# A diffusion block with three mixers: gate 1 in four column groups per step, gate 2 on VectorE, retention's heads in turn

## The chip, the cores and the metric

The kernel runs on one core of a Trainium2 chip. The metric is device time in microseconds (us), from the start to the end of one execution. Five engines work side by side on their own instruction queues: TensorE (PE in the profile; PEld is its weight load), VectorE (DVE), ScalarE (ACT), GpSimd (POOL) and SyncE (SP), which issues nearly all the DMAs here.

## What is computed

One block of a diffusion transformer for 256 latent and 256 context tokens of width 2048, in float32, shortened:

```python
m_lat = split(silu(c) @ ada_w + ada_b, 6)        # shift 1, scale 1, gate 1, shift 2, scale 2, gate 2
a_lat = modulate(x, norm1_g, m_lat[0], m_lat[1]) @ w_in      # a_ctx likewise for the context
hy, q, k, v, g, u = split_proj(a_lat)
mix = concat([hyena(hy), silu(g) * rms(retention(q, k, v)), s5(u)]) @ w_out
h = x + m_lat[2] * mix                                       # gate 1
up = modulate(h, norm2_g, m_lat[3], m_lat[4]) @ w_up         # shift 2, scale 2
gate, val = split(up, 2)
h = h + m_lat[5] * ((gelu(conv3x3(gate)) * val) @ w_down)    # gate 2
out = rmsnorm(h, norm_f)
```

Retention has eight heads of 64 query and key features and 128 value features. The modulation `ada_w` is a matrix of 2048 by 12288; its product with one vector takes no reuse of the weights at all.

## The kernel before

Weights come in blocks of 512 KB, 256 rows by 512 columns, into pages of 4 KB per partition. `split_w` (L449) loads a block, ACT rounds it to the high part (L454), DVE subtracts to get the low part (L456), and `prod` (L460) makes three PE products (L461 to L463) of each piece: high by high, high by low, low by high. Most blocks give 24 matmuls of 128 x 256 (blocks for keys of the context and for values also 128 x 512). PE cannot start on a block's second third before L456 is done. Pages for raw blocks, high and low parts and the modulation's loads are four rings of few pages each (the numbers in `RN`, and `resize`): a load into a page waits until the page's last reader is done.

Around the blocks runs other work, cut into steps by Python generators (`_Task`, L195). After each block a function `during_kv`, `during_g`, `during_hy` or `with_ada` asks each task for so many steps (`RK`, `RV`, `RG`, `RH`, `RW`, `RF`; broken rates add up). A timeline in the build then orders each engine's instructions by priority and its own estimate of when they can run; on the chip each engine goes through its list strictly in order.

One task is `ada25` (L443): the four chunks of the modulation that are needed late, 2048 columns each, in the order gate 1, shift 2, scale 2, gate 2 (chunks 0 to 3). Each takes 32 loads of 512 KB. A chunk in `ADV` goes to `ada_vector` (L419): DVE multiplies a load of 128 x 1024 with the vector's element on each partition and adds it to a sum (L428 for the first, L430 for the 15 others of a half), and PE sums over the partitions at the end of each half (L435). Any other chunk goes to `ada_matmul` (L404): PE multiplies the vector, 32 columns wide with the value in the first, into 512 columns of weights at a time (L412). The four groups of 512 columns lie side by side, on 32 of PE's columns and 32 partitions of one bank each. `ada_store` copies the sums out, transposes them (L397) and adds the bias (L400).

The order of the stages: S5 input and norm 1; keys and values of retention (with the S5 scan beside them); gates and queries; the hyena inputs, with retention's heads and the first part of hyena beside them; the output projection, 32 blocks, whose last quarter of each sum needs hyena's result; gate 1 and the residual (L1342); norm 2 (L311 to L321, L1354 to L1356 for the modulation by scale 2 and shift 2); and the feed-forward net (FFN): 11 groups of 512 gate columns (8 blocks), the convolution by nine taps on ACT and DVE (L1388, L1396), 512 value columns (8 blocks), their product (L1403) and its split in two parts (L466, L467), and the products down, which add gate 2 times the sum to the residual (L1419). The first product down comes after the third group up.

In before, gate 1 is made on PE from 163 us on, shift 2 and scale 2 on DVE from 333 to 558, gate 2 on PE from 576 to 728, all by L412 and L430 in the spaces between.

Retention (L1150) goes over four pairs of heads: per head two score matmuls into one bank (L1158, 64 rows of PE's 128, the lower for the first head of a pair and the upper for the second), the decay on DVE (L1161), the values (L1164).

Of the kernel before, what the change touches and what calls it, by code (L numbers as in the profile page):

```python
# [16 lines left out]
P = 128  # L17
D = 2048
KT = D // P
L = 256  # L20
# [36 lines left out]
def _lay(i):  # L57
    """The inputs as the kernel reads them: slices, transposes and constants of the shapes."""
# [70 lines left out]
    s = np.arange(256)  # L129
# [13 lines left out]
    # constants of the shapes  # L143
# [24 lines left out]
RN=[2,3,3,3];SA=40000;SF=30000;R0=10;R1=1;R2=1;RS=4;RK=2;RV=3;RG=.8;RH=.8;RW=.75;RF=.8;RT=1.2;RR=3;RY=.75;PR=500;ADV=[1,2];ORD=[0,1,2,3];RP=1.5;RQ=20;KS=5;PW=800;AR=[6,8,8,8,7,5,5,5];ZE=[1,3];VE=[0,1,3];UE=[1,3]  # L168
class _Pages:
    """Tags of fixed sizes in the slot pool, taken and given back in the order of the program."""  # L170
# [12 lines left out]
class _Ring:  # L183
    """Tags taken in turn."""
# [9 lines left out]
class _Task:  # L194
    """Work that is emitted piece by piece between the blocks of the large products."""  # L195
# [23 lines left out]
def tile_dit(ctx: ExitStack, tc: tile.TileContext, I, out: bass.AP, dbg=None):  # L219
# [15 lines left out]
    def stream(name, start):  # L235
        """Instructions whose order of priority starts at -start and goes on from use to use."""
# [9 lines left out]
    def resize(kind, n):  # L246
        """A ring of n pages of 4 KB."""
        tags = ring[kind].tags
        while len(tags) < n:
            tags.append(pages.take(4))  # L250
        while len(tags) > n:
            pages.give(tags.pop())
# [53 lines left out]
    def sum_squares(ps, sq, first, last):  # L306
        """Sums over the partitions and parts of sq [P, n, w], a token on each partition."""
# [6 lines left out]
    def inv_rms(ps, n, w):  # L314
        """1/sqrt(sum/n + eps) of w tokens' sums, on all partitions."""
# [76 lines left out]
    def ada_store(c, ps):  # L392
        """Four rows of 512 columns to their places."""
# [10 lines left out]
    def ada_matmul(c):  # L404
        """2048 of the modulation's columns for the latents, as products of TensorE."""
        ps = ada_bank()
        for kt in range(KT):
            raw = [load_a(I["ada25"][c, kt, half]) for half in range(2)]
            for half in (1, 0):
                for e in range(2):  # L410
                    q = 2 * half + e
                    T.matmul(ps[32 * q:32 * q + 32, :], cs[:, kt, :], raw[half][:, e, :],  # L412
                             start=(kt == 0), stop=(kt == KT - 1), skip_group_check=True)
                if (kt, half) != (KT - 1, 0):
                    yield
# [1059 lines left out]
```

## Time and profile before

| | us |
|---|---|
| median of three executions | 1503.16 |
| lowest, highest | 1502.71, 1507.03 |
| the profiled execution | 1507.03 |
| its span, first to last instruction | 1506.4 |
| PE busy in it | 1459.1 |
| DVE busy | 1040.6 |
| ACT busy | 658.0 |

The profiled execution is the highest of the three. The mean granted clock of TensorE was 0.987 of full speed. A row of the profile names line, engine, operation, output and inputs with shapes and how many; lengths are those of the records, which overlap a little on one engine, while the busy time of a window counts overlapping records once. A matmul in float32 leaves two records, a matmul of the split parts one. The idle time in brackets is the engine's idle time ahead of that row with what ended it.

### The profile page before, as it was taken

What the parts mean: (1) busy time and instruction counts of PE and PEld (TensorE: products, weight loads), DVE (VectorE), ACT (ScalarE), POOL (GpSimd) and SP (SyncE); (2) the same over time, 40 slices, a digit from 0 to 9 for tenths busy, and PEclk for the clock granted to TensorE, in tenths of its full rate; (3) what the DMA queues carried; (4) which work ended last, traced back from release to release, by engine and by line L of the source; (5) the groups of instructions that cost most, each with busy time, mean ns of one, the idle gap of its engine ahead of it and who ended that gap; (6) DMA issues with size and microseconds to landing.
All of it is one profiled execution on the core that took longest, in us unless ns stands there. A gap on an engine that the chain in (4) does not pass through costs nothing.

```text
span 1506.4 us, 27320 instructions
## 1 busy us (share of the span) xinstructions
PE 1459.1 (97%) x11180; PEld 1314.7 (87%) x11180; DVE 1040.6 (69%) x1772; ACT 658.0 (44%) x974; POOL 10.9 (1%) x9
## 2 busy tenths in 40 slices
PE   6998999999999999999999999999999999999997
PEld 3566687678888987788899999999999999999997
DVE  6579519897869887653777665775667577657756
ACT  6337741213576433232554443443444344434434
POOL 0000000000000000000000000000000000000000
PEclk9999999999999999999999999999999999999998
DMA  9788635568877887677465666556665666656562
GB/s 352 260 313 291 229 101 197 183 194 278 281 252 253 299 303 261 219 226 251 145 182 183 185 182 184 185 177 192 183 183 182 182 183 183 185 183 184 178 189 90
DMA packets 89956, 318.58 MB, mean 211 GB/s; under 512 B 12039, under 2 KB 12584, under 8 KB 89384
## 3 DMA queue, kind: packets, MB, share of 16 engines
q1 hardware_dynamic: 89832, 316.85, 65.4%
q8 instruction: 87, 1.43, 0.4%
q14 instruction: 37, 0.30, 0.1%
HBM read 312.62 MB, written 4.19 MB: 210 GB/s over the span
## 4 chain that ended last, share of the span: by engine, by line
PE 83%; DVE 7%; DMA 5%; ACT 3%; issue 1%; SPq 0%; DVEq 0%; ACTq 0%
PE mm L461 24%; PE mm L462 23%; PE mm L463 23%; DMA s4k<-in_ada_dram 4%; PE ad L412 4%; DVE s4k L456 1%; DVE s4k L430 1%; PE sm L852 1%; PE ad L373 1%; PE sm L576 1%; PE mm L339 1%; PE sm L546 1%; DMA s4k<-in_x_t_dram 1%; PE sm L1158 0%; PE sm L1164 0%
## 5 line engine op out<-in xcount | busy, mean ns | idle before, releaser
L456 DVE TENSOR_TENSOR s4k<-s4k,s4k 128x1024 fp32r<-128x1024 f32 x376 | 459.6, 1223 | 324.1 <-ACT s4k L454 300.5
L454 ACT CAST s4k<-s4k 128x1024 fp32r<-128x1024 f32 x376 | 393.8, 1048 | 654.7 <-PE mm L462 483.3
L462 PE MATMUL mm<-s4k,s4k 128*128 128x256 f32 (+1 forms) x2144 | 629.0, 294 | 1.5 <-DVE s4k L775 1.2
L461 PE MATMUL mm<-s4k,s4k 128*128 128x256 f32 (+1 forms) x2144 | 626.9, 295 | 3.5 <-ACT s4k L454 3.1
L463 PE MATMUL mm<-s4k,s4k 128*128 128x256 f32 (+1 forms) x2144 | 624.7, 294 | 3.2 <-DVE s4k L456 3.2
L461 PEld LDWEIGHTS mm<-s4k,s4k 128*128 128x128 f32 x2144 | 411.9, 193 | 27.3 <-issue 12.9
L462 PEld LDWEIGHTS mm<-s4k,s4k 128*128 128x128 f32 x2144 | 414.3, 193 | 18.4 <-issue 8.2
L463 PEld LDWEIGHTS mm<-s4k,s4k 128*128 128x128 f32 x2144 | 412.1, 193 | 17.2 <-issue 6.9
L461 PE MATMUL mm<-s8k,s4k 128*128 128x256 f32 x960 | 272.7, 285 | 0.0
L462 PE MATMUL mm<-s8k,s4k 128*128 128x256 f32 x960 | 271.7, 284 | 0.0
L463 PE MATMUL mm<-s8k,s4k 128*128 128x256 f32 x960 | 271.1, 284 | 0.0
L461 PEld LDWEIGHTS mm<-s8k,s4k 128*128 128x128 f32 x960 | 183.9, 192 | 14.4 <-issue 12.6
L463 PEld LDWEIGHTS mm<-s8k,s4k 128*128 128x128 f32 x960 | 183.7, 192 | 4.3 <-issue 3.4
L462 PEld LDWEIGHTS mm<-s8k,s4k 128*128 128x128 f32 x960 | 184.3, 192 | 2.7 <-issue 2.5
L1396 DVE SCALAR_TENSOR_TENSOR t<-mm,s4k,t 128x189 f32<-128x189 f32 (+2 forms) x352 | 131.9, 424 | 7.9 <-ACT t L1388 6.3
L430 DVE SCALAR_TENSOR_TENSOR s4k<-s4k,cs,s4k 128x1024 f32<-128x1024 f32 x60 | 76.8, 1280 | 21.0 <-DMA s4k<-in_ada_dram 20.4
L412 PE MATMUL ad<-s4k,cs 128*32 128x512 f32 x256 | 62.7, 612 | 1.0 <-DMA s4k<-in_ada_dram 1.0
L1419 DVE SCALAR_TENSOR_TENSOR s4k<-mm,ada_cols,s4k 128x256 f32<-128x256 f32 x96 | 39.9, 477 | 4.7 <-PE mm L463 4.7
L373 PE MATMUL ad<-s4k,cs 128*32 128x256 f32 x512 | 35.6, 392 | 4.7 <-DMA s4k<-in_ada_dram 4.0
L1388 ACT ACTIVATE t<-mm,s4k 128x256 f32<-128x256 f32 x44 | 24.7, 562 | 14.6 <-PE mm L463 13.6
L466 ACT CAST s8k<-t 128x512 fp32r<-128x512 f32 x38 | 23.0, 616 | 18.2 <-DVE t L1403 9.3
L373 PEld LDWEIGHTS ad<-s4k,cs 128*32 128x32 f32 x512 | 13.8, 110 | 19.1 <-DMA s4k<-in_ada_dram 5.7
(281 smaller groups left out, 1023.5 us busy)
## 6 DMA issues: line engine op xcount, KB each, us to landing
s4k<-in_ada_dram SPq DMA_DIRECT2D x192, 512.0 KB, 4.9
s4k<-in_w_up_dram SPq DMA_DIRECT2D x176, 512.0 KB, 3.7
s4k<-in_w_down_dram SPq DMA_DIRECT2D x88, 512.0 KB, 3.7
s4k<-in_w_in_dram SPq DMA_DIRECT2D x80, 512.0 KB, 4.9
s4k<-in_w_out_dram SPq DMA_DIRECT2D x32, 512.0 KB, 4.6
s4k<-in_x_t_dram SPq DMA_DIRECT2D x8, 512.0 KB, 6.6
s4k<-in_ctx_t_dram SPq DMA_DIRECT2D x4, 512.0 KB, 10.2
hyk<-s8k SPq DMA_DIRECT2D x4, 512.0 KB, 4.0
```

The lines of the kernel that those rows point to most:

```text
L373: T.matmul(ps[32 * q:32 * q + 32, :], cs[:, 2 * k2 + e, :], raw[:, e, 256 * part:256 * part + 256], start=(k2 == 0), stop=(k2 == 7), skip_ ...
L412: T.matmul(ps[32 * q:32 * q + 32, :], cs[:, kt, :], raw[half][:, e, :], start=(kt == 0), stop=(kt == KT - 1), skip_group_check=True)
L430: V.scalar_tensor_tensor(acc, raw, cs[:, kt, 0:1], acc, ALU.mult, ALU.add)
L454: S.copy(h, raw)
L456: V.tensor_tensor(lo, raw, h.bitcast(F32), ALU.subtract)
L461: T.matmul(ps, a[0], b[0], start=first, stop=False, skip_group_check=True)
L462: T.matmul(ps, a[0], b[1], start=False, stop=False, skip_group_check=True)
L463: T.matmul(ps, a[1], b[0], start=False, stop=last, skip_group_check=True)
L466: S.copy(h, src)
L1388: S.activation(acc[:, e, :], at(m), AF.Identity, bias=cw[:, 9, mt:mt + 1], scale=cw[:, 4, mt:mt + 1])
L1396: V.scalar_tensor_tensor(dst[:, r0:r1, c0:c1], src[:, r0 + dy:r1 + dy, c0 + dx:c1 + dx], cw[:, tap, mt:mt + 1], dst[:, r0:r1, c0:c1], ALU. ...
L1419: V.scalar_tensor_tensor(h_of(mt), at(m), ada_cols[:, 3, mt:mt + 1], h_of(mt), ALU.mult, ALU.add)
```

## The change

Three edits in the code, and numbers in the parameter line. `ada_matmul` issues all four column groups of a row tile in one step, from two loads, and hands back control once per row tile (16 steps) instead of once per load (32). `ADV` takes chunk 3, gate 2, to DVE. Retention takes a second bank per pair of heads and issues the scores so that the two heads take turns. Of the numbers, `RN` gives the modulation three pages instead of two in the stage of keys and values; a `resize` afterwards takes it back to two before gates and queries. `RK` goes from 2 to 1, `RV` from 3 to .5 and `RW` from .75 to .85, with which gate 1's 16 steps come beside the 24 blocks of keys and values, 8 beside the keys and 8 beside the values. Comments are left out too, which moves line numbers: L412 becomes L410, L428 and L430 become L426 and L428, L454 and L456 become L452 and L454.

```diff
-RN=[2,3,3,3]; ... RK=2;RV=3; ... RW=.75; ... ADV=[1,2];
+RN=[3,3,3,3]; ... RK=1;RV=.5; ... RW=.85; ... ADV=[1,2,3];
...
             raw = [load_a(I["ada25"][c, kt, half]) for half in range(2)]
-            for half in (1, 0):
-                for e in range(2):
-                    q = 2 * half + e
-                    T.matmul(ps[32 * q:32 * q + 32, :], cs[:, kt, :], raw[half][:, e, :],
-                             start=(kt == 0), stop=(kt == KT - 1), skip_group_check=True)
-                if (kt, half) != (KT - 1, 0):
-                    yield
+            for q in range(4):
+                T.matmul(ps[32 * q:32 * q + 32, :], cs[:, kt, :], raw[q // 2][:, q % 2, :],
+                         start=(kt == 0), stop=(kt == KT - 1), skip_group_check=True)
+            if kt < KT - 1:
+                yield
...
+    resize("ada", 2)
     tag_sg = pages.take(8)
...
             yb = sm_bank()
+            pss = [sm_bank(), sm_bank()]
+            for s in range(2):
+                for e in range(2):
+                    ph = slice(64 * e, 64 * e + 64)
+                    T.matmul(pss[e][:, L * s:L * s + L], k_t[ph, pr, 128 * s:128 * s + 128], q_t[ph, pr, :],
+                             start=True, stop=True)
             for e in range(2):
                 hd = 2 * pr + e
-                ph = slice(64 * e, 64 * e + 64)
-                ps = sm_bank()
-                for s in range(2):
-                    T.matmul(ps[:, L * s:L * s + L], k_t[ph, pr, 128 * s:128 * s + 128], q_t[ph, pr, :],
-                             start=True, stop=True)
+                ps = pss[e]
```

With the four chunks' steps changed in number (128 before, 112 after), they also fall on other stages: gate 1 alone goes with keys and values, shift 2 and scale 2 with gates, queries, hyena and the output projection, and gate 2 with the first two groups up of the FFN.

Where the instructions stand is told by each engine's list. The first place is on DVE in the FFN, before: the end of the first group up (L1403 and L467) and, from the row that ends in `s4k_1066_7697` on, the split of the blocks of the second group up.

```order
L1396 SCALAR_TENSOR_TENSOR t_7304<-mm_7027,s4k_989_7022,t_7304 128x3x63
L1403 TENSOR_TENSOR t_7284<-t_7284,mm_7324 128x512
L456 TENSOR_TENSOR s4k_1064_7669<-s4k_1062_7665,s4k_1063_7667 128x1024
L1403 TENSOR_TENSOR t_7304<-t_7304,mm_7325 128x512
L467 TENSOR_TENSOR s8k_991_7025<-t_7284,s8k_991_7025 128x512
L467 TENSOR_TENSOR s8k_991_7025<-t_7304,s8k_991_7025 128x512
L456 TENSOR_TENSOR s4k_1067_7699<-s4k_1065_7695,s4k_1066_7697 128x1024
L456 TENSOR_TENSOR s4k_1070_7729<-s4k_1068_7725,s4k_1069_7727 128x1024
```

After, the same place, the last row being the split of the second group's first block:

```order
L1397 SCALAR_TENSOR_TENSOR t_7173<-mm_6910,s4k_961_6906,t_7173 128x3x63
L1397 SCALAR_TENSOR_TENSOR t_7193<-mm_6911,s4k_961_6906,t_7193 128x192
L428 SCALAR_TENSOR_TENSOR s4k_1048_7610<-s4k_1099_8043,cs,s4k_1048_7610 128x1024
L1397 SCALAR_TENSOR_TENSOR t_7193<-mm_6911,s4k_961_6906,t_7193 128x3x63
L1404 TENSOR_TENSOR t_7173<-t_7173,mm_7213 128x512
L428 SCALAR_TENSOR_TENSOR s4k_1048_7610<-s4k_1106_8085,cs,s4k_1048_7610 128x1024
L1404 TENSOR_TENSOR t_7193<-t_7193,mm_7214 128x512
L465 TENSOR_TENSOR s8k_963_6909<-t_7173,s8k_963_6909 128x512
L428 SCALAR_TENSOR_TENSOR s4k_1048_7610<-s4k_1113_8148,cs,s4k_1048_7610 128x1024
L465 TENSOR_TENSOR s8k_963_6909<-t_7193,s8k_963_6909 128x512
L428 SCALAR_TENSOR_TENSOR s4k_1048_7610<-s4k_1117_8181,cs,s4k_1048_7610 128x1024
L454 TENSOR_TENSOR s4k_1052_7618<-s4k_1050_7614,s4k_1051_7616 128x1024
```

Between the last taps and that split now stand the steps of gate 2 that sum the loads into `s4k_1048`; in before the list has no step of the modulation there.

The second place is on DVE in hyena, beside the output projection. Before, at the end of hyena's first filter (L1252, L1256), with splits of `w_out` blocks between:

```order
L467 TENSOR_TENSOR s8k_718_5044<-t_5238,s8k_717_5043 128x512
L467 TENSOR_TENSOR s8k_718_5044<-t_5239,s8k_717_5043 128x512
L456 TENSOR_TENSOR s4k_862_6101<-s4k_860_6097,s4k_861_6099 128x1024
L1252 SCALAR_TENSOR_TENSOR t_5431<-s4k_634_4550,pk,sm_5406 128x256 x2
L1256 TENSOR_TENSOR s4k_716_5042<-t_5431,s4k_635_4551 128x512
L1252 SCALAR_TENSOR_TENSOR t_5497<-s4k_634_4550,pk,sm_5472 128x256 x2
L1256 TENSOR_TENSOR s4k_716_5042<-t_5497,s4k_635_4551 128x512
L456 TENSOR_TENSOR s4k_867_6137<-s4k_865_6133,s4k_866_6135 128x1024
L467 TENSOR_TENSOR s4k_786_5536<-sm_5537,s4k_785_5535 128x512
L467 TENSOR_TENSOR s4k_786_5536<-sm_5544,s4k_785_5535 128x512
```

After, the same place (L1253, L1257):

```order
L428 SCALAR_TENSOR_TENSOR s4k_737_5324<-s4k_820_5941,cs,s4k_737_5324 128x1024
L1287 SCALAR_TENSOR_TENSOR s4k_599_4441<-mm_5233,pk,s4k_599_4441 128x255
L465 TENSOR_TENSOR s8k_681_4933<-t_5128,s8k_680_4932 128x512
L428 SCALAR_TENSOR_TENSOR s4k_737_5324<-s4k_824_5974,cs,s4k_737_5324 128x1024
L428 SCALAR_TENSOR_TENSOR s4k_737_5324<-s4k_828_6007,cs,s4k_737_5324 128x1024
L428 SCALAR_TENSOR_TENSOR s4k_737_5324<-s4k_835_6070,cs,s4k_737_5324 128x1024
L1253 SCALAR_TENSOR_TENSOR t_5319<-s4k_597_4439,pk,sm_5294 128x256 x2
L1253 SCALAR_TENSOR_TENSOR t_5383<-s4k_597_4439,pk,sm_5358 128x256 x2
L428 SCALAR_TENSOR_TENSOR s4k_737_5324<-s4k_839_6103,cs,s4k_737_5324 128x1024
L1257 TENSOR_TENSOR s4k_679_4931<-t_5319,s4k_598_4440 128x512
L1257 TENSOR_TENSOR s4k_679_4931<-t_5383,s4k_598_4440 128x512
L426 TENSOR_SCALAR s4k_843_6138<-s4k_844_6139,cs 128x1024
```

Six steps of scale 2 now stand in these twelve rows, and the splits of the `w_out` blocks come behind them.

The third place is PE in the key and value stage, at gate 1. Before, each pair of column groups stands by itself among the products:

```order
L461 MATMUL mm_2535<-s4k_387_2799,s4k_102_629 128x512
L462 MATMUL mm_2535<-s4k_388_2801,s4k_102_629 128x512
L412 MATMUL ad_1937<-s4k_366_2711,cs 32x512 x2
L463 MATMUL mm_2535<-s4k_387_2799,s4k_103_630 128x512
L461 MATMUL mm_2536<-s4k_387_2799,s4k_102_629 128x512
L462 MATMUL mm_2536<-s4k_388_2801,s4k_102_629 128x512
L463 MATMUL mm_2536<-s4k_387_2799,s4k_103_630 128x512
L461 MATMUL mm_2533<-s4k_398_2857,s4k_132_879 128x512
L412 MATMUL ad_1937<-s4k_365_2709,cs 32x512 x2
L462 MATMUL mm_2533<-s4k_399_2859,s4k_132_879 128x512
```

After, the two pairs of a row tile are adjacent:

```order
L460 MATMUL mm_2536<-s4k_380_2771,s4k_102_629 128x512
L461 MATMUL mm_2536<-s4k_379_2769,s4k_103_630 128x512
L410 MATMUL ad_1937<-s4k_387_2815,cs 32x512 x2
L410 MATMUL ad_1937<-s4k_388_2817,cs 32x512 x2
L459 MATMUL mm_2533<-s4k_390_2825,s4k_132_879 128x512
L460 MATMUL mm_2533<-s4k_391_2827,s4k_132_879 128x512
L461 MATMUL mm_2533<-s4k_390_2825,s4k_133_880 128x512
```

Other row tiles read alike; a few in before already had their pairs adjacent.

## Rows read from the trace of the kernel before

**Rows 1.** The page's first part: the span, and each engine's busy time.

```profile
span 1506.4 us, 27320 instructions
...
PE 1459.1 (97%) x11180; PEld 1314.7 (87%) x11180; DVE 1040.6 (69%) x1772; ACT 658.0 (44%) x974; POOL 10.9 (1%) x9
```

**Rows 2.** Windows: length, busy (records) of PE, PEld, DVE, ACT, POOL; PEclk, DMA, GB/s.

```profile
333.00:475.00 142.00, 131.21 (x929) 121.99 (x927) 112.61 (x168) 82.60 (x145) 7.19 (x4) 0.98 0.80 271
475.00:566.00 91.00, 90.76 (x666) 83.16 (x665) 76.76 (x93) 33.89 (x42) 0.00 (x0) 1.00 0.85 285
566.00:650.00 84.00, 83.63 (x561) 64.45 (x559) 54.29 (x84) 26.33 (x36) 0.00 (x0) 1.00 0.71 238
726.80:790.00 63.20, 62.62 (x493) 61.12 (x489) 49.64 (x89) 32.99 (x45) 0.00 (x0) 0.95 0.50 152
790.00:1490.00 700.00, 700.00 (x5836) 700.00 (x5835) 472.52 (x698) 303.19 (x339) 0.00 (x0) 1.00 0.60 180
```

**Rows 3.** Line L412 (gate matmul on PE), all of it: duration min/median/max.

```profile
L412 PE MATMUL ad<-s4k,cs x256: 592/616/1063, 163.2 to 727.1; 128*32 128x512 f32 x128
```

**Rows 4.** PE in order of time: start, length, work; one pair of L412.

```profile
664.87 0.28 PE L463 MATMUL mm<-s8k,s4k 128*128 128x256 f32 x1
665.07 1.05 PE L412 MATMUL ad<-s4k,cs 128*32 128x512 f32 x4
666.06 0.38 PE L461 MATMUL mm<-s8k,s4k 128*128 128x256 f32 x1
```

**Rows 5.** PE in order of time: two pairs of L412 side by side.

```profile
212.88 1.07 PE L412 MATMUL ad<-s4k,cs 128*32 128x512 f32 x8
213.88 0.39 PE L461 MATMUL mm<-s4k,s4k 128*128 128x256 f32 x1
```

**Rows 6.** PE in order of time, at norm 2.

```profile
726.62 1.05 PE L412 MATMUL ad<-s4k,cs 128*32 128x512 f32 x4 [0.21 <-DMA s4k<-in_ada_dram]
727.60 1.10 PE L321 MATMUL sm<-ident,t 128*128 128x128 f32 x4
```

**Rows 7.** DVE in order of time, at norm 2, with idle time and releaser.

```profile
726.80 0.18 DVE L318 RECIPROCAL t<-t 128x4 f32<-128x4 f32 x1 [2.91 <-ACT t L317]
728.75 1.66 DVE L1354 SCALAR_TENSOR_TENSOR t<-s4k,ada_cols,sm 128x256 f32<-128x256 f32 x4 [1.77 <-PE sm L321]
```

**Rows 8.** Line L1158, the score matmuls of retention.

```profile
L1158 PE MATMUL sm<-s4k,s4k x32: 375/376/481, 473.2 to 559.0; 64*128 64x256 f32 x32
```

**Rows 9.** Line L430 on DVE, and its idle time before it (us, times).

```profile
L430 DVE SCALAR_TENSOR_TENSOR s4k<-s4k,cs,s4k x60: 1266/1282/1287, 333.1 to 557.0; 128x1024 f32<-128x1024 f32 x60
...
  DMA s4k<-in_ada_dram: 20.4, 21
```

**Rows 10.** DVE in order of time, where L430 stands densest.

```profile
344.57 2.61 DVE L430 SCALAR_TENSOR_TENSOR s4k<-s4k,cs,s4k 128x1024 f32<-128x1024 f32 x2 [0.72 <-DMA s4k<-in_ada_dram]
...
352.55 1.29 DVE L430 SCALAR_TENSOR_TENSOR s4k<-s4k,cs,s4k 128x1024 f32<-128x1024 f32 x1 [0.94 <-DMA s4k<-in_ada_dram]
353.75 1.22 DVE L456 TENSOR_TENSOR s4k<-s4k,s4k 128x1024 fp32r<-128x1024 f32 x1
...
361.54 1.27 DVE L430 SCALAR_TENSOR_TENSOR s4k<-s4k,cs,s4k 128x1024 f32<-128x1024 f32 x1
```

**Rows 11.** Line L430, from 333 to 430 alone.

```profile
L430 DVE SCALAR_TENSOR_TENSOR s4k<-s4k,cs,s4k x30: 1266/1284/1287, 333.1 to 429.0; 128x1024 f32<-128x1024 f32 x30
```

**Rows 12.** DMA issues: count, KB each, median us to landing.

```profile
s4k<-in_ada_dram SPq DMA_DIRECT2D x192, 512.0 KB, 4.9
s4k<-in_w_up_dram SPq DMA_DIRECT2D x176, 512.0 KB, 3.7
```

**Rows 13.** PE in order of time: the second up product's first matmul.

```profile
790.00 0.28 PE L461 MATMUL mm<-s4k,s4k 128*128 128x256 f32 x1
```

**Rows 14.** The page's costliest lines: busy, mean ns, idle before, releaser.

```profile
L456 DVE TENSOR_TENSOR s4k<-s4k,s4k 128x1024 fp32r<-128x1024 f32 x376 | 459.6, 1223 | 324.1 <-ACT s4k L454 300.5
...
L1396 DVE SCALAR_TENSOR_TENSOR t<-mm,s4k,t 128x189 f32<-128x189 f32 (+2 forms) x352 | 131.9, 424 | 7.9 <-ACT t L1388 6.3
```

More of the change, by code (lines that the diff above doesn't have):

```diff
@@ L165, in _lay @@
     return o
-RN=[2,3,3,3];SA=40000;SF=30000;R0=10;R1=1;R2=1;RS=4;RK=2;RV=3;RG=.8;RH=.8;RW=.75;RF=.8;RT=1.2;RR=3;RY=.75;PR=500;ADV=[1,2];ORD=[0,1,2,3];RP=1.5;RQ=20;KS=5;PW=800;AR=[6,8,8,8,7,5,5,5];ZE=[1,3];VE=[0,1,3];UE=[1,3]
+RN=[3,3,3,3];SA=40000;SF=30000;R0=10;R1=1;R2=1;RS=4;RK=1;RV=.5;RG=.8;RH=.8;RW=.85;RF=.8;RT=1.2;RR=3;RY=.75;PR=500;ADV=[1,2,3];ORD=[0,1,2,3];RP=1.5;RQ=20;KS=5;PW=800;AR=[6,8,8,8,7,5,5,5];ZE=[1,3];VE=[0,1,3];UE=[1,3]
 class _Pages:
```

## The prediction

> **What bounds the kernel now.** I read the page's first table first: TensorE (PE) is busy 1459.1 of a span of 1506.4 us, VectorE (DVE) 1040.6 [rows 1]. So time is saved where PE has less to do, as long as DVE follows. Next the windows by stage [rows 2]: from 475 on PE hardly has a gap (90.76 of 91.00, 83.63 of 84.00, 700.00 of 700.00); 333 to 475 leaves it idle for 10.8 us. There one microsecond taken from PE is one microsecond off the end, until DVE or a load comes later than PE. The same rows show the reserve on DVE: 54.29 of 84.00 in the stretch of hyena with the first half of the output projection (566 to 650), 49.64 of 63.20 between norm 2 and the second up product's first columns (726.8 to 790). The change puts its new DVE work into just these two. Third, the lines of the gate work itself, L412 on PE and L430 on DVE.
>
> **What goes from PE.** L412 is one pair of matmuls, two column groups of one load. In PE's own order one pair stands between two products at 665.07; products without one start 0.12 apart (700 us for 5836 records, [rows 2]), here they start at 664.87 and 666.06, 1.19 apart, so a run of one pair costs 1.07 [rows 4]. Four groups in a row, at 212.88, hold the next product back by 1.00 from their own start [rows 5]. Four groups on four column strips thus cost what two cost, and the edit of gate 1 is worth one run for each that falls away. In before, gate 1's 32 pairs stand in 26 runs (several pairs are adjacent already, as at 212.88); in after's PE order they stand in 20. Six runs less: 6 x 1.07 = 6.4 us. The change's words promise 16 of 32.
>
> Gate 2's pairs leave PE altogether: 27 runs, 16 of them in 566 to 650, x 1.07 = 28.9 us. Of the 256 records of L412 [rows 3] (two a matmul) they are half. In exchange PE sums gate 2 over partitions once per half: two more pairs of L435, of the same shape as L412's and taken at 1.0 each: +2.0.
>
> At norm 2 a pair of gate 2 runs at 726.62 and the transposes of L321 come at 727.60 [rows 6], for which DVE's first L1354 waits 1.77 [rows 7]. Without the pair they can start some 0.7 earlier: -0.7.
>
> Retention: 32 records of score matmuls, 376 ns each [rows 8]. They ran two by two on the same 64 rows of the array and now alternate between the lower and the upper 64. No row of before shows two halves at work side by side. From above: if they overlapped fully, at most half of 32 x 0.376 = 12 would go, -6. Below nothing: both score banks are taken before the first one's DVE product, so each of the eight heads can wait for a bank by about a record, 8 x 0.376 = +3. I take -2, nearer to no change because records of one pair overlap in PE's pipeline already, and keep both ends.
>
> Sum on PE: -6.4 - 28.9 + 2.0 - 0.7 - 2 = -36.0. Moving chunks 1 and 2 out of 333 to 475, where PE was idle for those 10.8, may return some of that; I count -1. Together -37.
>
> **What comes to DVE.** 32 steps of gate 2, 30 of them L430 (L428 in after, x90 in place of x60), on 128 x 1024. A record lasts 1282 ns [rows 9], but the next operation starts 0.08 before it ends: L430 at 352.55, L456 behind it at 353.75, 1.20 net [rows 10]. 32 x 1.20 = 38 us, which DVE has free over the kernel as a whole. Two things speak against taking that as hidden.
>
> First, a step has its own load of 512 KB, and the ring from which loads are taken has two pages in this part (after gives the third page of the key stage back before the gate and query stage). Step n+2 can load only when step n is done. The row for L430 says that DVE stood idle 20.4 us, 21 of 60 times, for such a load [rows 9]. In 333 to 430 the 30 steps take (429.0 - 333.1) / 29 = 3.3 each [rows 11], with other DVE work between; the densest stretch, from 344.57 to 361.54, has six steps in 16.97, 2.83 each, much of it in waits for loads [rows 10]. Loads of the modulation land in 4.9 at the median, of the up weights in 3.7 [rows 12]: with two pages (4.9 + 1.3) / 2 = 3.1 and (3.7 + 1.3) / 2 = 2.5. Bounds: 2.5 to 3.3; I call the pace p and take 3.0, between the two rows that show steps in a row.
>
> Second, DVE does its work in order, and what stands behind a step waits with it: above all L454 (L456 in before), without which PE has no low part of a block.
>
> (a) In the FFN, 27 of the 32 steps stand between norm 2's reciprocal (L318) and the split of weight block 20, with which the gate columns of the second up product begin. In before that block's first matmul starts at 790.00, 63.2 after 726.80 [rows 7, 13]. In after the split ends at 2.9 (an estimate for the first load, which is asked for shortly before L318 and has to land) + 26p + 1.2 + 1.2 (the last step and the split): 79, 83 and 91 for p = 2.83, 3.0 and 3.3. The lower bound is DVE's own work without any wait, each record less 0.08: 16 splits x 1.14, 32 taps x 0.345 [rows 14], 32 modulating operations x 0.39 (four in 1.66, [rows 7]), four products half as wide as a split x 0.6 and 27 x 1.20 make 18.2 + 11.0 + 12.5 + 2.4 + 32.4 = 76.5. So PE waits between 13 and 28; at p = 3.0 it is 20. The pile shown in the order, ten steps ahead of one split, is where it waits. I take 20.
>
> (b) In hyena and the output projection 28 steps stand between the split of block 76 and the last split of hyena's output, where before had five or fewer. DVE was busy 54.29 there [rows 2]: 54.3 + 28 x 1.20 = 87.9. PE's own need is 83.6 - 16 x 1.07 = 66.5; it can fall some 8 behind DVE's place in the order (three pages of split blocks, 2.9 each), which makes 75. Loss 13 by the sum; by the pace 28p - 75 = 4, 9 and 17. If all waits fall beside PE's own work: 0. Bounds 0 and 18, I take 11.
>
> The Trainium skill ("Trainium Kernel Development and Optimization", Best Practices) says to double-buffer so that loads run beside compute. By that rule two pages would be enough, a step would cost 1.20, and of (a) and (b) only DVE's own sums would be left, 13 + 13: -37 + 26 = -11, about 1492. The trace does not bear it out for these steps: 21 of 60 waited, 2.83 to 3.3 each, as shown above.
>
> **Sum.** -37 + 20 + 11 = -6. The profiled execution took 1507.0 (span 1506.4 and 0.6 around it); it would come to 1501. It lies 3.9 above the median of the runs, 1503.2, and the difference is carried over to that: 1497.
>
> **Rivals.** About 0.3% (4.5 us, outside 1498.7 to 1507.7) is what a measurement of this kernel tells from no change.
>
> DVE is not late: the steps find their loads landed and run in the idle time before L456, 324.1 over the kernel [rows 14]. Then PE's relief stays whole: 1503 - 37 = 1466. For it: DVE is at 69% only. Against: in the two stretches the plain sums exceed PE's need by 13 each, whatever the loads do. Its milder form (only the sums count) is the 1492 above. Chance of either 0.2, the full form 0.05 of that.
>
> Slower: the two-page ring. One mechanism: each step of gate 2 waits for a load that is asked for only when the step two before is done, and the splits behind wait with it. With p the two losses are 26p - 57.9 and 28p - 75, together 54p - 133; they reach 37 at p = 3.15. At 3.3, which the 30 steps of before show, they are 28 + 17 = 45: +8, about 1511; at 3.5, 1522. For it: the FFN already draws 170 to 180 GB/s [rows 2], so loads of weights and of the modulation share the queue; against: up weights land in 3.7, and the 3.3 contains other DVE work. Chance 0.22.
>
> The trade is even: what PE gives up returns as waits nearly to the microsecond (p near 3.1), because the four-group edit saves six runs and not sixteen. Time 1501 to 1507. Chance 0.2. The rest, 0.38, is the forecast with its own range, 1490 to 1500.
>
> **Numbers.** Faster: all of the forecast up to 1498.7 (0.34) and the first rival (0.2): 0.54. Same: the even trade and the forecast's upper edge: 0.24. Slower 0.22. Range for 8 in 10: the low end leaves out the whole relief (1479 means losses of 13 in all instead of 31); the high end takes in p = 3.3 and retention's worse bound: 1479 to 1514.
>
> **What would show it.** In after's trace: L410 with x128 instead of L412 with x256, in 20 runs of about 1.0. L428 x90 with idle time for modulation loads above 20.4, most of it new after 727; L454's wait there no longer for ACT but behind L428. PE idle between 727 and 810 about 20, and about 11 between 566 and 660, released by L454's low part; from the third up product on PE full as before. Score matmuls closer together. Wrong: if PE shows no gap in these two stretches (the first rival), if the gap in the FFN is above 28 (the pace is above 3.3), or if the stage before 475 changes by more than 5, which I have nearly left out.

## The result: 1.2% slower

| | before | after |
|---|---|---|
| median, us | 1505.1 | 1523.3 |
| lowest to highest | 1502.7 to 1507.1 | 1520.3 to 1523.7 |
| span of the profiled execution | 1506.4 | 1521.8 |

The ratio of after to before is 1.0117, with a 95% interval of 1.0099 to 1.0135. Forecast were 1497 and a range from 1479 to 1514. The page's first part, beside [rows 1]: PE does 32.5 us less, and the span is 15.4 longer.

```profile
span 1521.8 us, 27099 instructions
...
PE 1426.6 (94%) x11060; PEld 1318.9 (87%) x11060; DVE 1077.0 (71%) x1804; ACT 657.4 (43%) x974; POOL 10.9 (1%) x9
```

Both traces hold the same 9312 products of weight blocks, so they can be cut at the same product, and each stage compared:

| stage, and its start and end in before | before | after | difference | forecast |
|---|---|---|---|---|
| S5 input, almost all (0 to 164.6) | 164.6 | 161.7 | -2.9 | 0 |
| keys, values, half the gates (164.6 to 395.7) | 231.1 | 215.3 | -15.8 | -7.4 |
| gates, queries, first hyena inputs (395.7 to 486.6) | 90.9 | 92.7 | +1.8 | 0 |
| hyena inputs, hyena, output projection until hyena's result is used (486.6 to 656.3) | 169.7 | 181.2 | +11.4 | -8.1 |
| output projection, second half (656.3 to 714.1) | 57.7 | 47.2 | -10.5 | -11.8 |
| its last two blocks, norm 2 (714.1 to 729.8) | 15.7 | 19.5 | +3.8 | -0.7 |
| first two groups up of the FFN and most of the third (729.8 to 853.4) | 123.6 | 151.3 | +27.7 | +22 |
| the rest | 653.0 | 652.9 | 0 | 0 |

The 2.9 at the start belong to the execution of before that was profiled: `scores_only` below, which changes nothing there, is shorter by 2.6.

The windows of after, to be read beside [rows 2] (length, busy of PE, PEld, DVE, ACT and POOL, granted clock, DMA share, GB/s); the fourth runs from norm 2's reciprocal to the first matmul of the second up product:

```profile
475.00:566.00 91.00, 88.95 (x654) 82.73 (x653) 60.58 (x83) 36.81 (x49) 0.00 (x0) 1.00 0.63 212
566.00:650.00 84.00, 66.12 (x432) 62.15 (x433) 71.46 (x89) 20.08 (x25) 0.00 (x0) 0.84 0.78 254
650.00:721.00 71.00, 61.68 (x484) 58.82 (x483) 41.90 (x57) 26.96 (x34) 0.00 (x0) 0.92 0.63 191
712.16:790.44 78.28, 51.01 (x392) 49.01 (x393) 69.18 (x104) 25.43 (x37) 0.00 (x0) 0.83 0.80 268
790.44:1490.00 699.56, 699.56 (x5809) 698.59 (x5810) 474.41 (x694) 299.33 (x327) 0.00 (x0) 1.00 0.61 185
```

In both stretches to which DVE's new work went, DVE is now the busier engine, 71 of 84 and 69 of 78, and PE, which had no gap in before, stands idle for 18 and 27. From 790 on nothing has changed.

**The FFN.** PE in order of time at the largest gap:

```profile
770.01 1.05 PE L433 MATMUL ad<-s4k,ones 128*32 128x512 f32 x4
790.44 0.55 PE L459 MATMUL mm<-s4k,s4k 128*128 128x256 f32 x1 [19.38 <-DVE t L1397]
790.79 0.41 PE L460 MATMUL mm<-s4k,s4k 128*128 128x256 f32 x1
791.00 0.42 PE L461 MATMUL mm<-s4k,s4k 128*128 128x256 f32 x1
```

The first matmul of the second up product waits for L1397, the taps of the convolution, and not for a weight block. The four banks of `mm` hold the gate columns and the value columns of one group; the next group's gate columns need the first two again, and the taps read these. What stood ahead of the last taps on DVE at that time:

```profile
780.89 1.28 DVE L428 SCALAR_TENSOR_TENSOR s4k<-s4k,cs,s4k 128x1024 f32<-128x1024 f32 x1 [1.64 <-DMA s4k<-in_ada_dram]
782.09 1.44 DVE L1397 SCALAR_TENSOR_TENSOR t<-mm,s4k,t 128x189 f32<-128x189 f32 x4
783.45 1.27 DVE L428 SCALAR_TENSOR_TENSOR s4k<-s4k,cs,s4k 128x1024 f32<-128x1024 f32 x1
784.64 0.86 DVE L1397 SCALAR_TENSOR_TENSOR t<-mm,s4k,t 128x252 f32<-128x252 f32 x2
785.86 1.28 DVE L428 SCALAR_TENSOR_TENSOR s4k<-s4k,cs,s4k 128x1024 f32<-128x1024 f32 x1 [0.36 <-DMA s4k<-in_ada_dram]
...
799.60 1.28 DVE L428 SCALAR_TENSOR_TENSOR s4k<-s4k,cs,s4k 128x1024 f32<-128x1024 f32 x1 [0.83 <-DMA s4k<-in_ada_dram]
800.80 2.35 DVE L454 TENSOR_TENSOR s4k<-s4k,s4k 128x1024 fp32r<-128x1024 f32 x2
```

Steps and taps take turns, a step every 2.5 here. The banks came free 78.3 after norm 2's reciprocal (712.16 to 790.44). The 27th step behind the reciprocal starts at 799.60, and the split of block 20, of which the prediction spoke, follows at 800.80 and ends (at half of the 2.35) 89.8 after the reciprocal. From the first step at 715.34 (below) to the 27th it is (799.60 - 715.34) / 26 = 3.24 a step. From the reciprocal to the end of that split DVE is busy 78.3 of 89.8 and idle 11.5, of which 10.2 ahead of steps whose load is not in. So its own work alone would end some 15 behind the 63.2 of before, and the waits for loads make most of the rest (an estimate: no run here takes work and loads apart in the FFN).

**Norm 2.** DVE in order of time, beside [rows 7]: the step between the reciprocal and the first modulation waits for its load, and the modulation (L1355) with it, 4.4 after the reciprocal instead of 2.0. Two steps ahead of the reciprocal hold it up as well: its input from ACT (first row) is there at 710.05, and it starts 2.1 later; in before it follows its input at once.

```profile
709.79 0.26 ACT L317 ACTIVATE t<-sm,pk 128x4 f32<-128x4 f32 x1 [1.79 <-PE sm L311]
...
709.64 2.61 DVE L428 SCALAR_TENSOR_TENSOR s4k<-s4k,cs,s4k 128x1024 f32<-128x1024 f32 x2 [1.61 <-DMA s4k<-in_ada_dram]
712.16 0.17 DVE L318 RECIPROCAL t<-t 128x4 f32<-128x4 f32 x1
715.34 1.28 DVE L428 SCALAR_TENSOR_TENSOR s4k<-s4k,cs,s4k 128x1024 f32<-128x1024 f32 x1 [3.01 <-DMA s4k<-in_ada_dram]
716.54 1.65 DVE L1355 SCALAR_TENSOR_TENSOR t<-s4k,ada_cols,sm 128x256 f32<-128x256 f32 x4
```

**Hyena.** What PE waited for from 470 to 660 (us in total, times, longest); in before it was 0.6 in all:

```profile
PE sm L459 <- ACT s8k L464: 5.2, 2, 3.5
PE mm L459 <- ACT s8k L464: 5.2, 1, 5.2
PE mm L459 <- DVE s4k L1287: 2.7, 1, 2.7
PE mm L461 <- DVE s4k L454: 2.1, 2, 1.7
PE sm L459 <- DVE t L1230: 2.0, 1, 2.0
PE sm L461 <- DVE s8k L465: 1.9, 1, 1.9
```

Only 2.1 of it is for split blocks (L454), and 2.7 for a bank that the input convolution still reads (L1287). The rest is hyena's own chain, up to its result, in which PE's transforms (`sm`), DVE's products (L1229 to L1259) and the splits on ACT and DVE (L464, L465) follow each other. Term (b) of the prediction had the steps ahead of split blocks, of which PE has some in hand; the waits are for hyena's chain, of which it has none. The fourth stage of the table, cut at block 76 (549.7 in before, 543.7 in after), shows where the time goes:

```profile
469.60:543.70 74.10, 74.10 (x541) 68.65 (x541) 44.80 (x62) 29.06 (x39) 0.00 (x0) 1.00 0.54 178
543.70:650.80 107.10, 87.18 (x587) 82.12 (x586) 92.64 (x115) 29.47 (x37) 0.00 (x0) 0.87 0.81 269
```

The first part is 11.0 longer than in before, but PE is full in it: it holds 72 matmul records of retention's heads (L1156, L1165, L1167) where before had 46, and before had 20 of these behind block 76. All of PE's waits, 19.9, lie in the second part. There also 90 products start some 0.21 apart, at the lower clock, where before had 23: about 6 us more.

### The profile page after: what moved, and what is told of

It is laid out like the page before. It is cut to its first block, busy times and chain, and to the rows that moved or that the text cites. A ratio compares the mean times of both kernels' runs of the same rounds, so it can differ in the third digit from the quotient of the medians.

```text
span 1521.8 us, 27099 instructions
## 1 busy us (share of the span) xinstructions
PE 1426.6 (94%) x11060; PEld 1318.9 (87%) x11060; DVE 1077.0 (71%) x1804; ACT 657.4 (43%) x974; POOL 10.9 (1%) x9
## 4 chain that ended last, share of the span: by engine, by line
PE 75%; DVE 10%; DMA 9%; ACT 2%; issue 2%; SPq 0%; DVEq 0%
PE mm L461 22%; PE mm L460 22%; PE mm L459 22%; DMA s4k<-in_ada_dram 8%; DVE s4k L428 3%; DVE s4k L454 2%; PE ad L373 1%; PE sm L574 1%; PE ad L410 1%; PE sm L850 1%; ACT s4k L452 1%; PE sm L544 1%; PE mm L339 1%; DMA s4k<-in_x_t_dram 1%; PE sm L1165 0%
## 5 line engine op out<-in xcount | busy, mean ns | idle before, releaser
L454 DVE TENSOR_TENSOR s4k<-s4k,s4k 128x1024 fp32r<-128x1024 f32 x376 | 459.3, 1223 | 308.4 <-ACT s4k L452 304.6
L452 ACT CAST s4k<-s4k 128x1024 fp32r<-128x1024 f32 x376 | 393.8, 1048 | 626.7 <-PE mm L460 447.1
L459 PE MATMUL mm<-s4k,s4k 128*128 128x256 f32 (+1 forms) x2144 | 627.0, 295 | 26.4 <-DVE t L1397 19.4
L459 PEld LDWEIGHTS mm<-s8k,s4k 128*128 128x128 f32 x960 | 187.0, 195 | 10.0 <-ACT s8k L464 5.4
L461 PEld LDWEIGHTS mm<-s8k,s4k 128*128 128x128 f32 x960 | 186.6, 195 | 3.6 <-DVE s4k L454 2.6
L460 PEld LDWEIGHTS mm<-s8k,s4k 128*128 128x128 f32 x960 | 187.2, 195 | 1.0 <-DVE s8k L465 1.0
L428 DVE SCALAR_TENSOR_TENSOR s4k<-s4k,cs,s4k 128x1024 f32<-128x1024 f32 x90 | 115.1, 1279 | 35.9 <-DMA s4k<-in_ada_dram 35.4
L1397 DVE SCALAR_TENSOR_TENSOR t<-mm,s4k,t 128x189 f32<-128x189 f32 (+2 forms) x352 | 132.2, 424 | 7.5 <-ACT t L1389 6.1
L464 ACT CAST s8k<-t 128x512 fp32r<-128x512 f32 x38 | 23.3, 617 | 42.2 <-DVE t L1259 16.1
L465 DVE TENSOR_TENSOR s8k<-t,s8k 128x512 fp32r<-128x512 f32 x38 | 25.9, 685 | 1.6 <-ACT s8k L464 0.7
## 6 DMA issues: line engine op xcount, KB each, us to landing
s4k<-in_ctx_t_dram SPq DMA_DIRECT2D x4, 512.0 KB, 10.2
```

Of the source, the lines that this page charges most:

```text
L428: V.scalar_tensor_tensor(acc, raw, cs[:, kt, 0:1], acc, ALU.mult, ALU.add)
L452: S.copy(h, raw)
L454: V.tensor_tensor(lo, raw, h.bitcast(F32), ALU.subtract)
L459: T.matmul(ps, a[0], b[0], start=first, stop=False, skip_group_check=True)
L460: T.matmul(ps, a[0], b[1], start=False, stop=False, skip_group_check=True)
L461: T.matmul(ps, a[1], b[0], start=False, stop=last, skip_group_check=True)
```

## The experiments

Three theories. A: DVE does its list in order, and the moved steps stand ahead of work that PE needs at once. B: another part of the change costs (four-group matmuls, third page, scores). C, a rival to A on the mechanism: the loads on two pages set the pace, not DVE's work.

### Where the loss comes from

`narrow_h` and `one_load_h` take apart a step's work and its load, in the stretch of hyena. `narrow_h`:

```diff
-                    V.scalar_tensor_tensor(acc, raw, cs[:, kt, 0:1], acc, ALU.mult, ALU.add)
+                    n = 16 if c < 3 else 512
+                    V.scalar_tensor_tensor(acc[:, :, :n], raw[:, :, :n], cs[:, kt, 0:1], acc[:, :, :n], ALU.mult, ALU.add)
```

> After, with DVE's steps of shift 2 and scale 2 on 16 of 512 columns (the rest of these two chunks' sums is left out), all loads kept: about 1.1 us of DVE work less for each of 60 steps. Theory A (DVE's own work, in order ahead of hyena's chain, makes the loss of 28 in the stretch of blocks 72 to 106): the waits of PE there fall by most of 21, -15 to -20: 1503 to 1508. Rival C (the loads and their two pages set the pace): the waits stay, at most -6: 1517 to 1523.

`one_load_h`:

```diff
-                raw = load_a(I["ada25"][c, kt, half])
+                if c == 3 or kt == 0:
+                    raw = load_a(I["ada25"][c, kt, half])
```

> After, with the steps of shift 2 and scale 2 reading one load per half again and again (56 of 64 loads left out, so these sums are of other data), DVE's work kept. The list moves: 32 steps instead of 27 stand in blocks 80 to 96, gate 2's come before the FFN. Theory A (work): DVE has as much to do in the stretch of hyena, the waits of PE there stay within a third of after's 21. Rival C (loads): the waits there go under 5. For the FFN both say that its loss goes, since gate 2's steps are done by then: A 1495 to 1503 in all, C about 1480.

Measured: 1483.9 (ratio 0.9845, 0.9811 to 0.9880) and 1489.6 (0.9889, 0.9858 to 0.9919). The same 150 us window of after, `narrow_h` and `one_load_h`, and the steps in it (in the last two kernels they are line L429), in this order:

```profile
500.00:650.00 150.00, 130.08 (x898) 121.37 (x897) 117.43 (x150) 45.62 (x59) 0.00 (x0) 0.91 0.73 245
```

```profile
500.00:650.00 150.00, 150.00 (x1154) 142.97 (x1154) 104.94 (x170) 58.93 (x73) 0.00 (x0) 1.00 0.81 284
...
L429 DVE SCALAR_TENSOR_TENSOR s4k<-s4k,cs,s4k x30: 117/247/253, 536.6 to 641.8; 128x32 f32<-128x32 f32 x30
...
  DMA s4k<-in_ada_dram: 11.1, 12
```

```profile
500.00:650.00 150.00, 127.82 (x859) 116.22 (x859) 122.89 (x156) 44.00 (x58) 0.00 (x0) 0.89 0.64 203
...
L429 DVE SCALAR_TENSOR_TENSOR s4k<-s4k,cs,s4k x36: 1260/1278/1286, 500.8 to 649.7; 128x1024 f32<-128x1024 f32 x36
```

Of shift 2 and scale 2 `narrow_h` leaves out most of the columns and `one_load_h` most of the loads; neither computes them. With all 30 loads and hardly any work PE has no gap at all, at 284 GB/s, although DVE still waits 11.1 for loads. Without most of the loads of shift 2 and scale 2 (gate 2's stay, and DVE waits 6.8 for them), but with the work (36 steps here), PE stands idle for 22; in after it was 20. In hyena it is DVE's work that costs, and C is out there. `narrow_h` gained twice what was expected: cut at the same products, it is shorter than after by 32.8 where after lost 28, by 18.2 in the gates, queries and first hyena inputs, and longer by 19.4 ahead of these, where its list is another. The FFN, in which gate 2's steps keep their full width, is still 23.8 longer than in before. `one_load_h` also shows gate 2's steps done ahead of the FFN, in the second half of the output projection: 11 of them stand there and cost nothing (46.1 us against 47.2), and the FFN's loss is gone.

`gate2_only` puts gate 2 on DVE in before, nothing else:

```diff
-ADV=[1,2]
+ADV=[1,2,3]
```

> Before with gate 2 on DVE as the only edit: pairs of column groups for gate 1, two pages throughout, the old scores. Its 32 steps fall into hyena and the output projection, not into the FFN. Theory A: PE is relieved of 28.9, DVE gets 32 steps where 54 of 84 us were busy, 92 against PE's 66: loss of 26 to 36, no loss in the FFN: 1500 to 1511. Rival B (DVE's steps are harmless, other edits cost): 1475 to 1480.

Measured 1518.9, ratio 1.0094 (1.0068 to 1.0120): worse than A's range. From 486.6 to 656.3 of before it takes 24.4 longer, though PE was relieved of 17 there; the FFN is unchanged (-0.4). Its window shows the state of after (PE 130.08) once more, with other chunks:

```profile
500.00:650.00 150.00, 131.06 (x913) 117.81 (x913) 128.05 (x161) 48.72 (x63) 0.00 (x0) 0.93 0.83 279
```

So steps of gate 2 do in hyena what those of scale 2 do in after. Cut at the same products, the stage from 549.7 to 656.3 of before holds 3 steps there, with PE idle for 0.4; 30 in after (19.9); 35 in `gate2_only` (31.2); 37 in `one_load_h` (22.2); and 21 narrow ones in `narrow_h` (0).

`more_banks` is after with other banks for the value product:

```diff
-        bk2, at2 = gemm_feat(I["w_up"], NU + u, f_of, between)
+        bk2, at2 = gemm_feat(I["w_up"], NU + u, f_of, between, bank=sm_bank)
```

> After with the value product of each FFN group in two of the three other banks, so that the next group's gate columns needn't wait for the taps. Theory A, as read from the trace (the deadline that fails is the bank, held by the taps, 51.7 after norm 2's reciprocal, not the split of block 20 at 63.2): the step of 20.5 at that place becomes about 9, the 12 us that lie between the two deadlines: 1511 to 1514. Rival (the weight blocks themselves are late, because their loads stand behind the modulation's on SP's queue): the loss moves to the split and stays above 20: 1521 to 1525.

Measured 1508.4, ratio 1.0015 (0.9994 to 1.0036), 1% better than after. In the profiled execution, which is 4.9 below the median, the loss in the FFN falls from 27.7 to 9.4 (the kernel's time from norm 2's end on against before's), so more than the 12 came back. What PE still waited for there, from 700 to 830:

```profile
PE mm L459 <- ACT s4k L1356: 4.1, 1, 4.1
PE sm L461 <- DVE s4k L454: 3.4, 3, 2.1
PE sm L321 <- DVE t L318: 2.8, 1, 2.8
```

No wait for L1397 is left. The list is another too: with the banks free, the scheduler has 8 steps fewer ahead of the split of block 20 (19 and not 27 behind the reciprocal), and 14 of the 32 taps behind it. The bank and this order were not taken apart, so the expected 12 is not shown as such; shown is that with other banks, and the list that comes with them, two thirds of the loss go, while all 32 steps remain on DVE.

### The four column groups

`gate2_back` is after with gate 2 on PE again, in four groups:

```diff
-ADV=[1,2,3]
+ADV=[1,2]
```

> Gate 2 back on PE (in the four-group form), all else as after. Theory A (the 32 steps of gate 2 on DVE stand ahead of the taps that free the FFN's banks): the wait of 19.4 before the second up product goes, the loss of 27.7 in the FFN falls under 3 and the 3.8 at norm 2 to about 0; PE gets 16 runs of 1.0 back: 1523.5 - 26 - 3 + 16 = about 1510. The stretch of hyena stays as in after, since shift 2 and scale 2 stand where they did. Rival B (the four-group matmul, the third page or retention's scores do the harm): the loss stays and the time goes up by the 16: about 1539.

Measured 1533.0, ratio 1.0187 (1.0164 to 1.0209): near the figure of rival B, yet A's wait is gone (no wait of PE above 0.3 in the FFN up to 900). The miss is in the price of gate 2 on PE: the FFN is 27.1 longer than in before all the same, for 25 of gate 2's runs now stand in it (25 x 1.07 = 26.8). Its matmuls there:

```profile
743.80 1.05 PE L410 MATMUL ad<-s4k,cs 128*32 128x512 f32 x4
746.29 1.05 PE L410 MATMUL ad<-s4k,cs 128*32 128x512 f32 x4
```

Each x4 is one pair, as in [rows 4], and not the x8 of [rows 5]. There are two pages at that place: as soon as the first pair has read its page the next load goes there, the other comes later, and the scheduler lets each pair run when its load is in. `turns` begins the row tiles in turn with the second and the first load, meant so that the first pair waits for the load that lands last:

```diff
-            for q in range(4):
+            for q in ((2, 3, 0, 1) if c and kt % 2 == 0 else (0, 1, 2, 3)):
```

> The kernel with gate 2 back on PE (1533), and in it the four groups of gate 2 begin in turn with the second and the first load of a row tile, so that the load which lands last is waited for by the first pair and the list keeps all four side by side; nothing else changes. Theory A2 (on two pages the second load lands later than the first, so the four groups stand as two pairs at 1.07 each; 48 runs in that kernel's list, 35 with this edit): 13 runs less, 14 us: about 1519. Rival (four groups are slow in the FFN for another reason, the loads or the queue): within 4 of 1533.

Measured 1517.8, ratio 1.0080 (1.0050 to 1.0110), 1.07% or 16 us better than `gate2_back`: the size that A2 has. The trace has 35 runs in place of 48. Not all of the gain lies where they fell away, though: the profiled executions differ by 17.8, 6.0 of it in the FFN (11 runs less, and 3.0 of waits for loads) and 4.9 in norm 2; the rest comes ahead of gate 2 and is not explained. The same product's matmuls now:

```profile
784.38 1.06 PE L410 MATMUL ad<-s4k,cs 128*32 128x512 f32 x8
792.35 1.06 PE L410 MATMUL ad<-s4k,cs 128*32 128x512 f32 x8
```

`pages3` is before with the third page alone:

```diff
-RN=[2,3,3,3]
+RN=[3,3,3,3]
...
+    resize("ada", 2)          # ahead of gates and queries
```

> Before with one edit of the change: three pages for the modulation up to the end of keys and values, two after. By its list, gate 1 stands in 16 runs of four groups instead of 26 without any edit of its matmuls, gate 2 in 31 instead of 27. Theory A2 (a third page makes the runs of four; the form of the loop does not): -10 x 1.07 + 4 x 1.07 = -6, and -3 in norm 1, whose loads no longer wait: about 1496. Rival (the gain of 18.5 up to the end of keys and values in after comes from the steps of shift 2 that left that stage): no more than 2 faster, 1503 to 1505.

Measured 1505.8, ratio 1.0007 (0.9987 to 1.0027): no gain. A2's 1496 is missed; the rival's "no more than 2 faster" holds, though its cause is seen only in part. The trace has gate 1 in 16 runs of four groups, without the edit of the loop, and the stage from 164.6 to 395.7 is shorter by 8.0; but the next one takes 5.0 longer, and 2.1 more follow up to 549.7. So the third page does without the new loop what the loop was meant for (the loop on two pages was not run for gate 1), and by subtraction half of after's gain of 15.8 in that stage is not gate 1's. Most likely it comes with the steps that left it (23 there in before, 8 in after); that was not taken apart.

### Retention

`old_scores` is after with the scores head by head, `scores_only` before with the new order.

```diff
+            pss = [sm_bank(), sm_bank()]
+            for s in range(2):
+                for e in range(2):
+                    T.matmul(pss[e][:, L * s:L * s + L], k_t[64 * e:64 * e + 64, pr, ...], q_t[...], ...)
```

> After with retention's scores head by head as in before. Prediction's term: the new order is worth 2, so 1525; bounds 1520 to 1530. Rival: the two banks taken at once hold up PE or DVE in hyena, and without them 5 or more of the 11.4 lost there come back: under 1519.

> Before with retention's new order of scores as the only edit. The prediction's term is -2 with bounds -6 and +3; old_scores against after gave +2, less than the two intervals: 1501 to 1503. Rival (two banks at once hold up hyena): 1506 or more.

Measured 1525.5 (ratio 1.0136, 1.0113 to 1.0159; after's is 1.0117) and 1509.6 (1.0018, 0.9997 to 1.0040). No gain can be measured in either direction; the forecast of -2 lies just outside `scores_only`'s interval (-0.5 to +6). But the edit reached PE's list for one pair of heads only. The matmuls and the next product behind them, before first, then after:

```profile
473.24 1.13 PE L1158 MATMUL sm<-s4k,s4k 64*128 64x256 f32 x4
474.30 0.39 PE L463 MATMUL mm<-s4k,s4k 128*128 128x256 f32 x1
```

```profile
456.38 1.14 PE L1156 MATMUL sm<-s4k,s4k 64*128 64x256 f32 x8
457.44 0.39 PE L459 MATMUL mm<-s4k,s4k 128*128 128x256 f32 x1
...
481.06 1.13 PE L1156 MATMUL sm<-s4k,s4k 64*128 64x256 f32 x4
482.12 0.39 PE L460 MATMUL mm<-s4k,s4k 128*128 128x256 f32 x1
```

Where the two heads take turns, their eight records hold the next product back by 1.06 from their own start, as one head's four do: the two halves of 64 rows work side by side. In the other three pairs each head's four records stand by themselves, as in before, and in `scores_only` it is the same. So one time in four the full gain came, about 1 us, which is too little to measure here; what parted the other three pairs is not shown.

### Versions meant to be faster

`best2` keeps what paid: gate 1 in fours on three pages, gate 2 on PE in fours, shift 2 and scale 2 where before had them.

```diff
-ADV=[1,2,3] ... RK=1;RV=.5 ... RW=.85
+ADV=[1,2] ... RK=2;RV=2 ... RW=.75
...
-            for q in range(4):
+            for q in ((0, 1, 2, 3) if kt % 2 and c else (2, 3, 0, 1)):
```

> A version meant to be faster than both: gate 2 on PE in four groups with the pages in turn, gate 1 in four groups on three pages, shift 2 and scale 2 on DVE where before had them (rates 2 and 2 in keys and values). 32 runs of L410 instead of 53 before: -22; the third page from the start -3, scores -2; DVE's steps as in before, so no new wait: 1503 - 27 = 1476 (bounds 1470 to 1485). If a new wait appears at hyena all the same: 1490 or more.

Measured 1488.9, ratio 0.9879 (0.9848 to 0.9910): faster than before by 1.2% and than after by 2.3%. All of L410 stands in 32 runs. It missed 1476 by 13. Keys and values are 8.0 shorter, 486.6 to 656.3 of before 7.1 and the second half of the output projection 4.2, together 19 of the 22 that were counted for the runs; of the 5 for the third page ahead and the scores hardly any came, and before itself measured 2.6 above the 1503 from which the sum started.

`best3` puts scale 2 on PE as well (`ADV=[1]`):

> As best2, but scale 2 too goes to PE in four groups; DVE keeps shift 2 alone. PE has 16 to 19 runs more, +19; DVE has 32 steps less in gates, queries and hyena, where best2 still has 10 more in blocks 60 to 72 than before. If DVE is what PE waits for there (theory A), the waits of 10.0 in that stretch and some of hyena's go: 1489 + 19 - 15 = 1493 (1485 to 1498). Rival (PE bounds the stretch): 1489 + 19 = 1508.

Measured 1506.7, ratio 1.0007 (0.9985 to 1.0028): the rival's figure. Without DVE's steps PE bounds the stretch, and its 19 us count in full; there scale 2 is better left to DVE.

`held` is `best2` with gate 2 on DVE, its steps held back until hyena is done, and the banks of `more_banks`:

```diff
+        while c == 3 and not t_hy.done:
+            yield
...
+            V.scalar_tensor_tensor(r4(col), hyd["mix"][:, :, :, 0:2].bitcast(F32), 0.0, r4(cs[:, :, 0]), ALU.mult, ALU.add)
```

> A version meant to be faster than best2 (1489): gate 2 on DVE as in the change, but its steps take their factor from a copy that is made only when hyena's result is there, so none can stand in hyena's stretch; in the FFN the value products use the other banks (as more_banks); shift 2 and scale 2 where best2 has them, gate 1 in runs of four. Theory A (DVE's steps cost only where DVE is what PE waits for, in hyena and ahead of the taps that free the banks): PE loses 16 runs, -17, two pairs of partition sums +2, DVE has 38 us free in the second half of the output projection and takes some 13 steps there, 19 fall around norm 2 and the first group up, where they cost 3 to 10: 1477 to 1484. Rival (a step of DVE costs PE about what it saves, wherever it stands): 1487 or more.

Measured 1488.1, ratio 0.9893 (0.9860 to 0.9926), the same as `best2`. From 549.7 to 714.1 of before it is 12 shorter than `best2`, as A has it, with 13 steps in the second half of the output projection; but norm 2 takes 6.4 longer and the FFN about 5. At norm 2's reciprocal, ACT's input for it and then DVE:

```profile
697.10 0.26 ACT L317 ACTIVATE t<-sm,pk 128x4 f32<-128x4 f32 x1 [4.16 <-PE sm L311]
...
696.11 1.29 DVE L435 SCALAR_TENSOR_TENSOR s4k<-s4k,cs,s4k 128x1024 f32<-128x1024 f32 x1 [3.25 <-DMA s4k<-in_ada_dram]
697.97 1.28 DVE L435 SCALAR_TENSOR_TENSOR s4k<-s4k,cs,s4k 128x1024 f32<-128x1024 f32 x1 [0.57 <-DMA s4k<-in_ada_dram]
699.17 0.17 DVE L318 RECIPROCAL t<-t 128x4 f32<-128x4 f32 x1
701.08 1.28 DVE L435 SCALAR_TENSOR_TENSOR s4k<-s4k,cs,s4k 128x1024 f32<-128x1024 f32 x1 [1.74 <-DMA s4k<-in_ada_dram]
```

At norm 2 the loads do count: two steps wait 3.25 and 0.57 for theirs, so that the second still runs when the reciprocal's input is there (697.36), and the reciprocal starts 1.8 late; the step behind it waits 1.74 and holds up the modulation. Steps on DVE are free in the second half of the output projection, not around norm 2.

## Why the prediction was wrong

The step that failed is **(b)**, hyena and the output projection: 11 with bounds 0 and 18 were taken, 28.5 came (11.4 longer in place of 17.1 shorter): 19.9 of waits, all behind block 76, some 6 of products at the lower clock, which the term did not have, and a rest of 2 to 3 that is not traced. Of the two ways in which it was summed, DVE's own work was the right one, and the pace of the loads was not what counts (`narrow_h`). But the 8 us by which PE was allowed to fall behind were not there: they are split blocks in hand, and only 2.1 of the waits were for those; 15 were for hyena's chain, of which PE has nothing in hand. Without the 8 the prediction's own sum gives 87.9 - 66.5 = 21, near the 19.9.

**(a)**, the FFN: right in mechanism, too small in size. 20 was taken, with bounds 13 and 28; 27.7 came, 2 of it for the partition sums and some 2 for the lower clock behind the long wait. The pace was 3.24 a step, near the mean row of before (3.3, [rows 11]), and not the 3.0 that was chosen; with 3.24 the same formula puts the split at 89.5 (measured 89.8) and the loss at 26.3. What the step did not see is that another deadline comes first: the banks for block 16, which before reached at 778.5, 51.7 after the reciprocal. In before the last of the taps starts at 777.95, half a microsecond ahead of that block's product, a row that was not looked for. Here both deadlines were missed by about the same, 26.6, so the error cost nothing.

**Norm 2**: -0.7 forecast, +3.8 measured. The order showed the step that now stands between reciprocal and modulation; that its load comes late (2.4), and that two steps ahead hold up the reciprocal (2.1), was left out of this term.

**What goes from PE.** Gate 2's 28.9: 10.5 of the expected 11.8 are seen in the rest of the output projection, the other 17.1 are in (b). The runs were miscounted: in the trace of before gate 2 stands in 30 and not 27, and after has gate 1 in 18 and not 20, so the relief was some 5 x 1.07 = 5 us larger than the sum says, and the losses with it. Partition sums came as forecast. Gate 1: 6.4 was counted for 6 runs; `pages3`, with 10 runs less, gained 8.0 in that stage. The -1 for shift 2 and scale 2 leaving 333 to 475 was too small: the stage up to 395.7 got 15.8 shorter in all, of which the runs of gate 1 are about half. That a change of more than 5 ahead of 475 would be a sign of being wrong, the prediction had said itself. Retention's -2 did not show: the two halves do work side by side, but in one pair of heads of four.

**The sum.** By stages (the table), measured less forecast: -2.9, -8.4, +1.8, +19.5, +1.3, +4.5, +5.7, together 21.5: 15.4 in place of -6. The rival that came true is the slower one, which gave 1511 at 3.3 a step: in the FFN with its own number (28), though loads and DVE's own work were not taken apart there, and in hyena with 28 in place of 17 and for another cause, since its loads did not set the time there. It too was 12 short of the 1523.

The Trainium skill's rule on double-buffering ("Trainium Kernel Development and Optimization", Best Practices), weighed in the prediction, gave 1492 there and was set aside for the 21 waits of 60. Such waits were there (14.0 from 500 to 650, 11 times), but with nearly as many (11.1, 12 times) and hardly any work on DVE PE had no gap in `narrow_h`; so neither the rule's sum nor the row that was set against it was what decided in hyena.

## What to carry to other kernels

An engine at 69% over the whole kernel can be the bound in the very stage to which work is moved: take its list there, in order, and ask for each instruction behind the new ones which engine waits for it and whether that engine has anything in hand. Deadlines are not only data: a bank or page that must be free again can come due before the next operand. Matmuls that are to run side by side need their loads to land together; with too few pages the list pulls them apart, and the order shows it before any run. That an edit puts instructions side by side in the code does not mean that they stand so in the list: of the four pairs of heads one did.

## What was unexpected of the hardware

After the wait of 19.4 in the FFN PE ran at the lower of its two levels, 1.2 instead of 2.4 GHz: products start 0.21 apart (790.79, 791.00) in place of 0.12, some 20 of them, about 2 us; the granted clock from norm 2's reciprocal to there is 0.83, and 0.95 in before [rows 2]. In hyena's stretch, with 19.9 of waits in 107.1 and a granted clock of 0.87, 90 products start so, about 6 us more than in before. Waits of PE thus cost more than their own length. In `narrow_h` weight and modulation loads together moved 284 GB/s over 150 us with PE without a gap, so the 245 GB/s of after in that window are not the limit of the loads.
